# The account that orders the instructions of a two-stack transformer kernel charges each operation another duration

## The chip, the cores and the metric

The kernel runs on one NeuronCore of a Trainium2 chip. A core has five engines with instruction streams of their own: TensorE (PE, the matrix multiplier), VectorE (DVE), ScalarE (ACT), GpSimd (POOL) and SyncE (SP, which here only issues transfers). Each engine works through its instructions strictly in the order in which they were built, and an instruction that has to wait for another engine holds up everything behind it on its own. The metric is the device time of one launch in microseconds (us).

## The reference, cut to what matters

Two stacks are computed one after the other, in float32, on 512 tokens of 1024 channels (`second` gets the output of `first`, and 256 context tokens of its own).

```python
# first stack: two layers
x = x + gated_deltanet(rmsnorm(x), ...)      # layer 0: projections, a causal convolution of 4 taps,
                                             # chunks of 64 tokens, a triangular solve, a scan over 8 chunks
x = x + swiglu(rmsnorm(x), w_in, w_out)
x = x + dilated_attention(rmsnorm(x), ...)   # layer 1: 3 groups of 8 heads
x = x + swiglu(rmsnorm(x), w_in, w_out)

# second stack: two layers, each
h, hc = modulate(x, ...), modulate(ctx, ...)             # layer norm, scale and shift
qa, ka, va, zb, qc, kc, vc = split(h @ w_in)             # the same for hc
o_a = neighbourhood_attention(qa, ka, va, context, rpb)  # 6 heads
o_b = spatial_gating(gelu(zb), w_s, b_s, g_sgu)
o_c = attend(rope(rms(qc) * g_q), rope(rms(kc) * g_k), vc, context)
y = concat(rms(o_a), rms(o_b), rms(o_c)) @ w_o           # layer 0: also for the context
x = layer_norm(ALPHA * x + gate * y) ...                 # then a gated swiglu of the same kind
```

## The kernel before, in words

All activations stay on the chip, in blocks of 128 tokens (blocks 0 to 3 are the tokens, 4 and 5 the context). Weights are streamed in slabs of half a megabyte. A float32 product is made of three passes over rounded parts: `xh` times `wh`, `xl` times `wh`, `xh` times `wl`, where `h` is the rounded part of a number and `l` the rest. So each tile that goes into a product must first be rounded (ACT, `xh<-xn`) and have its rest taken (POOL, `xl<-xn,xh`), and each weight slab as well (ACT `whia`, `whib`; POOL `wloa`, `wlob`).

In time the program has eight stages: the gated delta net (0 to 440 us of the span), a feed-forward (to 870), the dilated attention (to 1130), a feed-forward (to 1480), the mixing sublayer of the second stack's first layer (to 1985), its feed-forward (to 2500), the mixing sublayer of its second layer (to 2905) and its feed-forward (to the end).

The order of the instructions is decided while the program is built, by the class `Weave`. The main thread writes the large products. Everything else is written by side chains, Python generators that are advanced a step at a time: a norm, a convolution, a softmax, a rotation. After every second matmul or so of a large product the main thread calls `tick`, which advances each side chain whose last result is ready, by the account, at least `MARGIN` (1000 ns) before PE's present time. The account is a clock for each engine, `t[PE]`, `t[DVE]`, `t[ACT]`, `t[POOL]`, and a time `ready` for each chain: `note` adds what `cost` charges for the instruction and, behind it, the hand-over `LAT`, which counts only where the chain's next instruction is on another engine. Where the main thread needs the result of a chain it calls `join`, and `advance` moves PE's clock on. No duration is measured at run time: a larger charge makes the account believe that a result comes later, so the chain's next step is written behind more matmuls. After this the tile framework still moves some instructions by a few places.

The places that the prediction speaks of: in the delta net, `conv` (line 680: three multiply-adds `kT<-m,cw,kT` that read a bank of PSUM, which the next large product needs), `blocks` (line 831: a recurrence of pairs `tmp<-Pk,T` and `T<-T,tmp`), `gram` (line 786); in the mixing sublayer, `modulate` (line 1773: `xn`, transposes `s<-ident,xn` on PE, scaling on ACT and DVE, `xh`, `xl`), `rope_T` (line 2107: `w2k` and its reciprocal root `rs_t`, `qrs` on DVE, then transposes `s<-ident,w2k` on PE), the tables `tqk` made from a load `w2k<-rope` (in `mix`, line 2025), `values` (line 2215) and `merge` (line 2195). All instructions pass through one helper and so have line 138 in the profile.

Of the kernel before, what the change touches and what calls it, by code (L numbers as in the profile page):

```python
# [121 lines left out]
def _free(ap):  # L122
    n = 1
    for s in ap.shape[1:]:
        n *= s
    return n
# [35 lines left out]
class Weave:  # L162


    LAT = 125.0
    MARGIN = 1000.0

    def __init__(self):
# [3 lines left out]
    def cost(self, e, op, a, k):  # L172
        out = a[0] if a else k["out"]
        if op == "dma_start":
            return "DMA", 2100.0 + _free(out) * 4 * out.shape[0] / 170.0
        if e == "PE":
            if op == "transpose":
                return e, 116.0
            n = _free(out)
            if a[1].dtype == F32R:  # L180
                return e, max(n * 0.4225, 116.0)
            return e, 1.7 * n
        n = max(_free(x) for x in a[:2] if hasattr(x, "shape"))
        if e == "DVE":
            return e, (75 if n < 64 else 120) + 1.04 * n
        if e == "ACT":
            return e, 100 + 0.85 * n
        return e, 100 + 2.2 * n

    def note(self, e, op, a, k):  # L190
        if e == "SP" and self.cur is None:
            return
        e, c = self.cost(e, op, a, k)
        s, t = self.cur, self.t
        if s is None:
            if e == "DMA":
                return
            t[e] = (t[e] if e == "PE" else max(t[e], t["PE"])) + c
        elif e == "DMA":
            s.ready += c  # L200
            s.eng = e
        else:
            start = t[e] if s.eng == e else max(t[e], s.ready)
            t[e] = start + c
            s.ready = t[e] + self.LAT
            s.eng = e

    def now(self):
# [2462 lines left out]
```

## Time and profile before

| | us |
|---|---|
| median of three runs | 3285.81 (3278.48 to 3289.23) |
| the profiled execution's own time | 3274.1 |
| its span | 3272.3 |
| PE busy | 3073.1 (94%) |
| DVE busy | 1633.1 (50%) |
| ACT busy | 1255.7 (38%) |
| POOL busy | 1705.2 (52%) |

The median is 11.7 us (0.36%) above the profiled execution, so sums made against the profile are carried over to the median as differences. Busy shares are means over eight stages; what a changed order is worth is to be read where PE, the busiest engine, stands still.

### The profile page before, as it was taken

The numbers are of one execution on the slowest core, as the hardware profiler recorded it, in microseconds if no ns is written. First come the engines' busy times: TensorE is split into PE (matmuls) and PEld (weight loads), VectorE is DVE, ScalarE is ACT, GpSimd is POOL, SyncE is SP. The second block draws the span as 40 slices with busy tenths as digits, with TensorE's granted clock in tenths as the row PEclk, the third lists the DMA queues.
The fourth block names the chain that finished last, engine by engine and source line by source line (L and its number), as shares of the span: only waits on it lengthen the run. The fifth ranks groups of instructions, "written<-read, shape, count | busy, mean of one in ns | idle before, by whom it ended". The sixth has DMA issues, their size and how long they took to land.

```text
span 3272.3 us, 46609 instructions
## 1 busy us (share of the span) xinstructions
PE 3073.1 (94%) x16596; PEld 2662.7 (81%) x16596; DVE 1633.1 (50%) x4221; ACT 1255.7 (38%) x2542; POOL 1705.2 (52%) x2163
## 2 busy tenths in 40 slices
PE   7899899999999899998998879999998899979997
PEld 6787788888999788888898768888887798868886
DVE  6886476666455674517546752021115855731113
ACT  4443332223444432235546534212122656452322
POOL 3424368774333396765534245444546624475665
PEclk9989899999999999999998889999999899989999
DMA  3212245553222455622111221122121112143231
GB/s 111 67 35 71 85 157 184 168 173 103 74 65 62 159 181 190 202 97 75 59 33 52 62 77 53 64 65 65 65 65 52 59 32 68 57 148 97 97 97 65
DMA packets 99467, 301.97 MB, mean 92 GB/s; under 512 B 18673, under 2 KB 26017, under 8 KB 99233
## 3 DMA queue, kind: packets, MB, share of 16 engines
q1 hardware_dynamic: 74000, 236.36, 22.3%
q10 hardware_dynamic: 25232, 62.62, 6.1%
q8 instruction: 131, 2.15, 0.3%
q14 instruction: 104, 0.84, 0.1%
HBM read 290.98 MB, written 7.95 MB: 91 GB/s over the span
## 4 chain that ended last, share of the span: by engine, by line
PE 54%; DVE 5%; ACT 2%; POOL 2%; issue 1%; DMA 1%; SPq 0%; ACTq 0%; DVEq 0%; POOLq 0%
PE b L138 28%; PE m L138 23%; PE s L138 4%; ACT xn L138 1%; DVE rs_t L138 1%; DVE w2k L138 1%; DVE x L138 1%; POOL wloa L138 0%; POOL xl L138 0%; DVE qrs L138 0%; ACT w2k L138 0%; POOL wlob L138 0%; DVE macc L138 0%; DVE xl L138 0%; DMA gr<-grow 0%
## 5 line engine op out<-in xcount | busy, mean ns | idle before, releaser
L138 POOL TENSOR_TENSOR wloa<-wrawa,whia 128x256 fp32r<-128x256 f32 x639 | 492.7, 802 | 515.8 <-ACT whia L138 479.2
L138 POOL TENSOR_TENSOR wlob<-wrawa,whib 128x256 fp32r<-128x256 f32 x475 | 364.6, 801 | 209.3 <-ACT whib L138 183.4
L138 DVE SCALAR_TENSOR_TENSOR th<-th,b 128x512 f32<-128x512 f32 x66 | 45.4, 687 | 611.1 <-ACT th L138 611.1
L138 ACT CAST whia<-wrawa 128x1024 fp32r<-128x1024 f32 (+2 forms) x164 | 168.2, 1027 | 379.6 <-PE m L138 202.8
L138 PE MATMUL m<-xh,whia 128*128 128x512 f32 (+1 forms) x760 | 269.8, 361 | 15.5 <-ACT xh L138 6.9
L138 PE MATMUL m<-xl,whia 128*128 128x512 f32 (+1 forms) x760 | 266.8, 357 | 13.9 <-POOL xl L138 13.8
L138 POOL TENSOR_TENSOR wloa<-wrawb,whia 128x256 fp32r<-128x256 f32 x232 | 192.2, 859 | 149.5 <-ACT whia L138 141.9
L138 ACT CAST whib<-wrawa 128x1024 fp32r<-128x1024 f32 (+1 forms) x123 | 125.5, 1022 | 350.4 <-PE m L138 162.0
L138 DVE SCALAR_TENSOR_TENSOR macc<-mw,cv,macc 128x1024 f32<-128x1024 f32 x140 | 235.1, 1719 | 9.2 <-DMA mw<-w_mod 8.8
L138 POOL TENSOR_TENSOR wlob<-wrawb,whib 128x256 fp32r<-128x256 f32 x239 | 192.4, 835 | 89.8 <-ACT whib L138 89.0
L138 PE MATMUL b<-xh,whib 128*128 128x512 f32 (+1 forms) x624 | 228.4, 372 | 1.4 <-ACT xh L138 1.4
L138 PE MATMUL b<-xl,whib 128*128 128x512 f32 (+1 forms) x624 | 227.4, 371 | 0.0
L138 PE MATMUL b<-xl,whia 128*128 128x512 f32 (+1 forms) x528 | 197.6, 378 | 2.8 <-POOL xl L138 2.8
L138 PE MATMUL b<-xh,whia 128*128 128x512 f32 (+1 forms) x528 | 198.0, 379 | 0.5 <-ACT xh L138 0.5
L138 POOL TENSOR_TENSOR hl<-th,hh 128x512 fp32r<-128x512 f32 (+1 forms) x110 | 158.1, 1446 | 69.8 <-ACT hh L138 67.3
L138 PE MATMUL m<-xh,wloa 128*128 128x512 f32 (+1 forms) x760 | 185.3, 354 | 0.0
L138 PEld LDWEIGHTS m<-xh,whia 128*128 128x128 f32 x760 | 145.4, 192 | 45.0 <-issue 8.4
L138 PEld LDWEIGHTS m<-xl,whia 128*128 128x128 f32 x760 | 145.2, 191 | 40.8 <-POOL xl L138 14.6
L138 PE MATMUL m<-whia,xh 128*128 128x512 f32 (+3 forms) x440 | 168.1, 385 | 5.7 <-ACT xh L138 3.2
L138 PE MATMUL m<-whib,xh 128*128 128x512 f32 (+3 forms) x432 | 162.1, 377 | 10.1 <-ACT xh L138 5.4
L138 PE MATMUL m<-whia,xl 128*128 128x512 f32 (+3 forms) x440 | 166.2, 380 | 3.8 <-POOL xl L138 3.3
L138 PE MATMUL m<-whib,xl 128*128 128x512 f32 (+3 forms) x432 | 161.7, 376 | 6.1 <-POOL xl L138 5.9
(457 smaller groups left out, 8043.3 us busy)
## 6 DMA issues: line engine op xcount, KB each, us to landing
mw<-w_mod ACTq DMA_DIRECT2D x96, 512.0 KB, 4.3
wrawa<-ffn_w_in SPq DMA_DIRECT2D x60, 512.0 KB, 3.4
wrawa<-w_ffn_in SPq DMA_DIRECT2D x56, 512.0 KB, 3.4
wrawa<-gdn_w_in SPq DMA_DIRECT2D x32, 512.0 KB, 3.4
wrawb<-w_ffn_in SPq DMA_DIRECT2D x32, 512.0 KB, 3.4
wrawa<-w_ffn_out SPq DMA_DIRECT2D x32, 512.0 KB, 3.4
wrawb<-ffn_w_in SPq DMA_DIRECT2D x28, 512.0 KB, 3.4
wrawa<-ffn_w_out SPq DMA_DIRECT2D x28, 512.0 KB, 3.5
```

The costliest lines, as they stand in the source:

```text
L138: r = f(*a, **k)
```

## The change

Two tables of numbers in `Weave` change. The hand-over, 125 ns behind every engine, becomes 250 ns behind PE and 60 ns behind the others. The fixed charge of an operation rises: on DVE from 75 ns (under 64 elements) or 120 ns to 155 ns, and 85 ns more with a running sum; on ACT from 100 to 150 ns, 60 ns more where the bias or the scale is a tile and 190 ns more with a running sum; on POOL from 100 to 180 ns. The charge of an element hardly changes (ACT 0.85 to 0.87 ns, POOL 2.2 to 2.18 ns, DVE 1.04 ns as before); PE's and the transfers' charges stay. No instruction is added or removed.

```diff
-    LAT = 125.0
+    LAT = {"PE": 250.0}
@@ cost()
-            return e, (75 if n < 64 else 120) + 1.04 * n
+            return e, 155 + 1.04 * n + (85 if total else 0)
         if e == "ACT":
-            return e, 100 + 0.85 * n
-        return e, 100 + 2.2 * n
+            vec = any(hasattr(k.get(x), "shape") for x in ("bias", "scale"))
+            return e, 150 + 0.87 * n + (60 if vec else 0) + (190 if total else 0)
+        return e, 180 + 2.18 * n
@@ note()
-            s.ready = t[e] + self.LAT
+            s.ready = t[e] + self.LAT.get(e, 60.0)
```

What this moves is seen in the built order. The four feed-forward stages keep theirs but for a few places at their seams, and the dilated attention nearly so. In the delta net and in both mixing sublayers large parts of it move. Three places follow.

The first is DVE in the delta net, about 130 to 135 us into the span of before: `T_282` and `tmp` are the recurrence of the first pair of heads, whose steps get shorter as it goes on (128x25x2, 128x24x2, ... 128x16x4, 128x15x5), and `qT<-m,cw,qT` is the convolution for the third pair. Before:

```order
L138 TENSOR_TENSOR T_282<-T_282,tmp 128x16x4
L138 TENSOR_TENSOR tmp<-Pk,T_282 128x75
L138 TENSOR_TENSOR T_282<-T_282,tmp 128x15x5
L138 SCALAR_TENSOR_TENSOR qT<-m,cw,qT 128x511
L138 TENSOR_TENSOR tmp<-Pk,T_282 128x70
L138 SCALAR_TENSOR_TENSOR qT<-m,cw,qT 128x510
L138 TENSOR_TENSOR T_282<-T_282,tmp 128x14x5
L138 SCALAR_TENSOR_TENSOR qT<-m,cw,qT 128x509
```

Now:

```order
L138 TENSOR_TENSOR T_282<-T_282,tmp 128x25x2
L138 TENSOR_TENSOR tmp<-Pk,T_282 128x48
L138 SCALAR_TENSOR_TENSOR qT<-m,cw,qT 128x511
L138 TENSOR_TENSOR T_282<-T_282,tmp 128x24x2
L138 SCALAR_TENSOR_TENSOR qT<-m,cw,qT 128x510
L138 TENSOR_TENSOR tmp<-Pk,T_282 128x69
L138 SCALAR_TENSOR_TENSOR qT<-m,cw,qT 128x509
```

The convolution stood behind the step of 15 and stands behind the step of 25 now, ten steps of the recurrence (twenty instructions) earlier against it.

The second is PE at the start of the first mixing sublayer: `m` are the products of a block with the weights of its keys and values (two slabs, `whia_111` with `wloa_112`, then `whia_109` with `wloa_110`), and `s<-ident,w2k` the transposes at the end of the rotation of context block 4. Before, all 24 products of block 0 and all 24 of block 1 stand ahead of it:

```order
L138 MATMUL m<-whia_109,xh_12034 128x256
L138 MATMUL m<-whia_109,xl_12035 128x256
L138 MATMUL m<-wloa_110,xh_12034 128x256 x4
L138 MATMUL s<-ident,w2k 128x128 x2
L138 MATMUL s<-ident,xn 128x128 x4
L138 MATMUL m<-whia_111,xh_12034 128x256
```

Now only the products with the first slab do:

```order
L138 MATMUL m<-whia_111,xh_12034 128x256
L138 MATMUL m<-whia_111,xl_12035 128x256
L138 MATMUL m<-wloa_112,xh_12034 128x256 x4
L138 MATMUL s<-ident,w2k 128x128 x2
L138 MATMUL m<-whia_109,xl_12035 128x256
L138 MATMUL m<-whia_109,xh_12034 128x256
```

So 23 products of the second slab have moved from ahead of the rotation's transposes to behind them. On POOL the rest `xl` of each block's second half has moved behind the rotation's multiplication by `g_k` in the same way.

The third is POOL at the start of the second mixing sublayer: `xl1` are rests of the context (`xn_21154` before and `xn_21191` now is block 5), `xl0` those of the tokens, and `tqk` the tables that need the load of `rope`. Before:

```order
L138 TENSOR_TENSOR xl1_21002<-xn_21091,xh1_21001 128x4x128 x2
L138 TENSOR_TENSOR xl1_21002<-xn_21154,xh1_21001 128x4x128 x2
L138 MEMSET zero_21335 128x1
L138 MEMSET va_21323 64x768
L138 TENSOR_TENSOR tqk_21337<-w2k_21342,g_q_21338 128x256
L138 TENSOR_TENSOR tqk_21337<-w2k_21342,g_k_21340 128x256
L138 TENSOR_TENSOR xl0_21000<-xn_21284,xh0_20999 128x4x128
L138 TENSOR_TENSOR tqk_21337<-w2k_21342,w2k_21344 128x256 x2
```

Now:

```order
L138 TENSOR_TENSOR xl1_21000<-xn_21091,xh1_20999 128x4x128 x2
L138 MEMSET zero_21337 128x1
L138 MEMSET va_21325 64x768
L138 TENSOR_TENSOR xl1_21000<-xn_21191,xh1_20999 128x4x128
L138 TENSOR_TENSOR tqk_21339<-w2k_21344,g_q_21340 128x256
L138 TENSOR_TENSOR tqk_21339<-w2k_21344,g_k_21342 128x256
L138 TENSOR_TENSOR tqk_21339<-w2k_21344,w2k_21346 128x256 x2
L138 TENSOR_TENSOR xl1_21000<-xn_21191,xh1_20999 128x4x128
L138 TENSOR_TENSOR xl0_20998<-xn_21288,xh0_20997 128x4x128 x2
```

The rest of block 5's second half stood ahead of the four table multiplications and stands behind them now, and so does the first half of block 0. On PE the transposes of block 5 have moved behind all 24 products of block 4, and on ACT the seven loads (the fifth is `rope`) ahead of the rounding of block 5's second half.

## Rows read from the trace of the kernel before

**Rows 1.** The page's head and its part on busy time.

```profile
span 3272.3 us, 46609 instructions
...
PE 3073.1 (94%) x16596; PEld 2662.7 (81%) x16596; DVE 1633.1 (50%) x4221; ACT 1255.7 (38%) x2542; POOL 1705.2 (52%) x2163
```

**Rows 2.** The page's chain of waits, by engine.

```profile
PE 54%; DVE 5%; ACT 2%; POOL 2%; issue 1%; DMA 1%; SPq 0%; ACTq 0%; DVEq 0%; POOLq 0%
```

**Rows 3.** Windows by stage: length, busy PE, PEld, DVE, ACT, POOL, clock, DMA share, GB/s.

```profile
0.00:440.00 440.00, 389.37 (x2350) 327.87 (x2350) 301.08 (x797) 184.64 (x463) 163.28 (x211) 0.95 0.23 77
440.00:870.00 430.00, 429.03 (x2001) 364.16 (x2000) 266.04 (x371) 132.94 (x203) 297.37 (x318) 1.00 0.47 149
...
1480.00:1985.00 505.00, 447.49 (x2729) 407.30 (x2728) 308.70 (x1097) 269.19 (x682) 213.20 (x342) 0.91 0.18 57
...
2500.00:2905.00 405.00, 352.64 (x2160) 318.91 (x2158) 275.54 (x940) 221.68 (x515) 199.91 (x293) 0.92 0.22 68
```

**Rows 4.** Groups of instructions: count, busy us, mean ns of one, idle before.

```profile
L138 DVE SCALAR_TENSOR_TENSOR th<-th,b 128x512 f32<-128x512 f32 x66 | 45.4, 687 | 611.1 <-ACT th L138 611.1
...
L138 DVE TENSOR_SCALAR rs_t<-rs,rs_x 128x1 f32<-128x1 f32 x138 | 36.0, 268 | 2.0
...
L138 POOL TENSOR_TENSOR wloa<-wrawa,whia 128x256 fp32r<-128x256 f32 x638 | 492.3, 803 | 503.6 <-ACT whia L138 479.2 <-PE m L138 20.6 <-issue 3.0
```

**Rows 5.** Windows of 20 us in the delta net.

```profile
120.00:140.00 20.00, 15.23 (x73) 11.74 (x72) 18.12 (x47) 9.20 (x26) 5.67 (x9) 1.00 0.23 79
140.00:160.00 20.00, 16.93 (x73) 13.11 (x71) 19.51 (x61) 7.88 (x12) 9.08 (x12) 1.00 0.27 86
```

**Rows 6.** Timeline of PE in the delta net: start, us, instruction, idle before.

```profile
127.41 0.47 PE L138 MATMUL m<-xh,whia 128*128 128x512 f32 x1 [1.78 <-DVE T L138]
...
155.03 0.47 PE L138 MATMUL m<-xh,whia 128*128 128x512 f32 x1 [1.34 <-DVE cx L138]
```

**Rows 7.** Timeline of DVE at the start of the first mixing sublayer.

```profile
1504.94 0.29 DVE L138 TENSOR_REDUCE qss<-w2k 128x2 f32<-128x128 f32 x1 [0.82 <-ACT w2k L138]
...
1509.43 1.21 DVE L138 SCALAR_TENSOR_TENSOR qrs<-rs_t,qrs 128x2 f32<-128x2 f32 x1
...
1513.59 0.16 DVE L138 TENSOR_TENSOR rs_t<-rs_t,rs_x 128x2 f32<-128x2 f32 x1
```

**Rows 8.** Timeline of POOL in the same stretch.

```profile
1506.85 3.77 POOL L138 TENSOR_TENSOR xl<-xn,xh 128x512 fp32r<-128x512 f32 x3
1512.30 0.46 POOL L138 TENSOR_TENSOR w2k<-w2k,g_k 128x128 f32<-128x128 f32 x1 [1.69 <-DVE rs_t L138]
```

**Rows 9.** Timeline of PE in the same stretch.

```profile
1517.48 0.44 PE L138 MATMUL s<-ident,w2k 128*128 128x128 f32 x2 [2.35 <-DVE xn L138]
```

**Rows 10.** Timeline of POOL at the start of the second mixing sublayer.

```profile
2534.35 2.52 POOL L138 TENSOR_TENSOR xl<-xn,xh 128x512 fp32r<-128x512 f32 x2 [2.90 <-ACT xh L138]
...
2544.92 0.72 POOL L138 TENSOR_TENSOR tqk<-w2k,g_q 128x256 f32<-128x256 f32 x1 [7.21 <-DMA w2k<-rope]
```

**Rows 11.** Timeline of PE in the same stretch.

```profile
2525.36 1.97 PE L138 MATMUL s<-ident,xn 128*128 128x128 f32 x8 [3.73 <-ACT xn L138]
...
2547.61 0.58 PE L138 MATMUL m<-whib,xl 128*128 128x256 f32 x1 [1.76 <-POOL xl L138]
```

**Rows 12.** Timeline of ACT's load of rope in the same stretch.

```profile
2541.14 0.44 ACTq L138 DMA_DIRECT2D w2k<-rope  x1
```

**Rows 13.** Windows at either clock in the same stretch.

```profile
2529.30:2534.60 5.30, 5.30 (x24) 5.24 (x24) 3.17 (x17) 3.02 (x7) 2.40 (x2) 0.50 0.08 26
2536.00:2538.50 2.50, 2.50 (x23) 2.50 (x22) 2.50 (x7) 2.07 (x2) 1.65 (x3) 1.00 0.00 0
```

**Rows 14.** Timeline of PE near the end of the first mixing sublayer.

```profile
1894.72 0.90 PE L138 MATMUL s<-ident,qa 128*128 128x128 f32 x3 [4.24 <-DVE qa L138]
```

**Rows 15.** Timeline of PE in the middle of the first mixing sublayer.

```profile
1849.73 1.11 PE L138 MATMUL b<-ident,w2k 128*128 128x128 f32 x4 [2.81 <-ACT w2k L138]
```

**Rows 16.** Timeline of PE near the end of the second mixing sublayer.

```profile
2861.34 0.55 PE L138 MATMUL s<-ident,qa 128*128 128x128 f32 x3 [2.20 <-DVE qa L138]
```

More of the change, by code (lines that the diff above doesn't have):

```diff
@@ L183, in cost @@
         n = max(_free(x) for x in a[:2] if hasattr(x, "shape"))
+        total = k.get("accum_out") is not None
         if e == "DVE":
-            return e, (75 if n < 64 else 120) + 1.04 * n
+            return e, 155 + 1.04 * n + (85 if total else 0)
         if e == "ACT":
-            return e, 100 + 0.85 * n
-        return e, 100 + 2.2 * n
+            vec = any(hasattr(k.get(x), "shape") for x in ("bias", "scale"))
+            return e, 150 + 0.87 * n + (60 if vec else 0) + (190 if total else 0)
+        return e, 180 + 2.18 * n
     def note(self, e, op, a, k):
```

## The prediction

> **What bounds the kernel now.** I read the page's busy times first. PE is busy 3073.1 of 3272.3 us [rows 1], and by the chain of waits the end also hangs on PE before any other engine, 54% against 5% for DVE [rows 2]. So a change of order can give back at most PE's idle time, 199.2 us, and costs whatever it adds to it. Where that time lies is told by the windows by stage [rows 3]: the feed-forward from 440 to 870 has 429.03 busy of 430.00, so nothing is to be had there (and its order stays); the delta net has 389.37 of 440.00 (50.6 idle, of which the start of the kernel is a part that no order changes), the first mixing sublayer 447.49 of 505.00 (57.5 idle), the second 352.64 of 405.00 (52.4 idle). These three stages, 160.5 us of idle PE, are also where the instructions move. The mixing sublayers show a granted clock of 0.91 and 0.92, against 1.00 in the feed-forward: beside the idle time they pay for stretches at 1.2 GHz. How dear these are is shown by two neighbouring stretches with the same kind of product [rows 13]: 24 instructions took 5.30 us at a granted clock of 0.50, 23 took 2.50 us at 1.00. A gap that is opened or closed is therefore worth up to about twice its length.
>
> **What the charges do.** The groups of instructions show how far the old charges were off [rows 4]: a multiply-add over 512 elements takes 687 ns (charged 120 + 532 = 652 before, 155 + 532 = 687 now), one step of a reciprocal root on one element 268 ns (76 before, 156 now), a POOL subtraction over 256 elements 803 ns (663 before, 738 now). But where a chain changes engine, the lower hand-over, 60 for 125 ns, takes back 65 of the 80 ns that a DVE operation gained. So chains that stay on DVE (the recurrence, the roots) are now held to be later, chains that hop from engine to engine about as late as before. No work is added, so each part below is a sum over PE's gaps.
>
> **Part 1, the delta net: -5 us.** From 120 to 160 us DVE is nearly full (18.12 and 19.51 of 20 us) and PE stands for 4.77 + 3.07 = 7.8 us [rows 5]. Most of that is four gaps ahead of the next large product, the first of 1.78 and the last of 1.34 us [rows 6]; at their mean, 1.56, they make 6.2 us. The product waits for a bank that a convolution on DVE has yet to read. In the new order the convolution stands ten steps of the recurrence earlier, so these gaps should nearly go. DVE does the same work in the same time, though: what is brought forward makes the recurrence late, and the transposes and solve behind it. I take -5, most of the four gaps. Below, it can be no better than the 7.8 us and a little of the clock, -10; above, if PE runs into the late recurrence by the length of the two convolutions put ahead of it (2 x 4 operations x 0.687 = 5.5), +5.
>
> **Part 2, start of the first mixing sublayer: +4 us.** PE came to the rotation's transposes of block 4 with all 48 products of blocks 0 and 1 done, and stood 2.35 us until 1517.48 [rows 9]. Now 23 of these products (2.5 us at full clock, 5.1 at half, by rows 13) stand behind the transposes, and PE waits there with work undone behind it: it comes some 3 us sooner, at 1512, waits, and still has the 23 to do. The chain on DVE that it waits for starts at 1504.94 [rows 7], and POOL's step of it at 1512.30 [rows 8]. It will be shorter than before. Its steps on two elements take 0.16 us at 1513.59 but 1.21 us at 1509.43 [rows 7], and the long ones lie beside the three subtractions that POOL does in 3.77 us from 1506.85 [rows 8]; two of those three have moved behind the chain, 2.5 us, in which a step now takes 0.16 instead of about 1.2, so the chain ends about 2.2 us sooner, near 1515.3. Then 0.4 for the transposes and about 4 for the 23 products makes 1519.7, where before everything was done at 1517.9: +1.8. Behind the 23 also stand the transposes of blocks 2 and 3, whose rests are then late by up to as much again; I take +4. Bounds: 0 (the shorter chain pays for all) and +9 (no shortening, all at half clock).
>
> The GPSIMD Engine Reference of the Trainium skill (Specifications) says that GpSimd's way into SBUF is shared with VectorE and that they get in each other's way when a DVE instruction has two SBUF inputs or runs in its two-port mode. That agrees with the rows just named, 1.21 against 0.16 us beside POOL's subtractions. It speaks against a fixed charge for DVE at all. By the rule alone the shorter chain would count in full and part 2 would be +2, and without it +6.
>
> **Part 3, start of the second mixing sublayer: +4 us.** On PE the transposes of block 5 ran at 2525.36 [rows 11]; they now follow all of block 4's products, which end at 2534.6 [rows 13], 9 us later. Scaling and rounding on ACT were ready only for POOL's subtraction at 2534.35 before [rows 10], so the first half loses some 5 us, not 9. POOL's second half now stands behind the tables, which waited until 2544.92 for the load [rows 10] that ACT issued at 2541.14 [rows 12], 3.8 us before. ACT issues it about 1 us sooner now, so the tables run from about 2544 to 2547 (4 x 0.72), the subtraction lands near 2548.3, and block 5's last 11 products come after that. Before, PE stood at that time too: block 0's products began at 2547.61, after a wait for POOL [rows 11]. So block 5 fills a gap that was there, and only the remainder, 2 to 5 us of products, is late, and block 1's half behind the rotation. I take +4; bounds 0 (all of it falls into the old gap) and +8 (the whole of the first half's delay and half of block 1's).
>
> **Part 4, end of the first mixing sublayer: -3 us.** PE stood 4.24 us ahead of the last merge [rows 14]. Now 10 more products of another block stand between; at the 0.214 us that one takes at full clock (429.03 / 2001, rows 3) they cover 2.1, and the clock has less cause to fall. Bounds -4 and 0.
>
> **Part 5, the middle of the mixing sublayers: +3 us.** Some waits get more cover, such as the 2.81 us for ACT at 1849.73 [rows 15], others less: several of the softmax chains in the first sublayer stand with 3 us of products between producer and consumer where there were 7 to 10. These chains are long, and I cannot price each. Bounds -6 (twice the gap shown) and +12 (the same number again in the other direction, doubled as at half clock). I take +3, nearer to zero than to the upper end, since each late chain also delays others that then wait less.
>
> **Part 6, the rest: 0.** Near the end of the second sublayer the 2.20 us [rows 16] are covered by 18 products (3.9 us), and block 1's second transposes go behind block 0's, which costs about as much: 0, between -2 and +2. The dilated attention and the feed-forwards keep their order.
>
> **The sum.** -5 + 4 + 4 - 3 + 3 + 0 = +3 us on the profiled execution's own 3274.1: 3277. The median of the runs shown is 11.7 higher, 3285.81, so the time to expect is 3289. All lower ends together are -22, all upper ends +36.
>
> **The rivals.** *The waits go.* The old charge of a DVE chain was a third of its price, so its consumers were written too early and PE stood; with the dearer charge they come later. For it: the delta net's gaps and the 2.81 and 4.24. Against it: chains that hop engines are charged as before, and most gaps of the mixing sublayers lie at starts and ends, where there is nothing to put between. Price: parts 1, 4 and 5 at their lower ends, 2 and 3 at +1 each: -10 - 4 - 6 + 2 = -18, so 3268.
> *POOL's queue stands.* In both starts a POOL instruction that waits (the tables for a load, 7.21 us [rows 10]; the multiplication for DVE, 1.69 us [rows 8]) now stands ahead of the rests that the products need. Once that wait ends later than PE's last product ahead of it, each us goes straight to the end, at half clock. Price: parts 2 and 3 at +9 and +8, 4 more for the products done at 0.50, the others as taken (-5): +16, so 3302. Against it: PE stood there anyway.
> *It charges what no trace shows.* A step that takes 0.16 or 1.21 us is charged 157 ns either way. The order is then another, not a better one, and the parts cancel: 3286.
>
> **How the numbers follow.** A measurement of this kernel can tell about 0.3% from no change, 9.9 us. My forecast and the last rival both lie within that; with their spread they hold 0.37. Faster by more, the first rival and the lower tail: 0.31. Slower, POOL's queue and the upper tail: 0.32. For 8 times in 10 I go to -26 and +31 around the median: 3260 to 3317, which leaves out about a tenth on either side; the forecast's own range is 3276 to 3296.
>
> **What would show it.** Part 1: the four gaps between 120 and 160 us gone and DVE still full. Part 2: PE's wait ahead of the rotation's transposes longer than 2.35, the steps of 1.2 us fewer. Part 3: POOL's tables ahead of a subtraction, and PE waiting for `xl` after block 4's products. Part 4: the 4.24 below 2.2. It is wrong if the feed-forwards differ, or if the delta net and the mixing sublayers all move in one direction by more than 10 us.

## The result and the profile after

The changed kernel takes 3319.82 us (median of six runs, 3316.45 to 3323.68), the kernel before, in the same series, 3276.89 (3273.59 to 3289.23). The ratio is 1.0122, with a 95% interval of 1.011 to 1.0134: slower by 42.9 us between the medians (the ratio is taken by rounds; 1.22% of 3276.89 is 40 us, so differences in us are good to a few us). The forecast was no change (+3 us), its range ended at 3317, and slower by over 0.3% had a chance of 0.32. The sum was wrong by 40 us: even all upper ends of its parts together, +36, don't reach what was measured.

The page's rows on the span, the busy times and the chain, in the changed kernel [rows 1, 2]:

```profile
span 3321.9 us, 46617 instructions
...
PE 3097.9 (93%) x16596; PEld 2686.5 (81%) x16596; DVE 1643.5 (49%) x4221; ACT 1259.3 (38%) x2542; POOL 1711.5 (52%) x2163
...
PE 54%; DVE 5%; ACT 3%; POOL 2%; DMA 1%; issue 1%; ACTq 0%; SPq 0%; DVEq 0%; POOLq 0%
```

The span grew by 49.6 us (its own time is 3323.68, the slowest of its six). Every engine ran the same number of instructions of work, yet PE is busy 24.8 us longer, and idle 224.0 instead of 199.2, which is another 24.8. So in these two executions half of the loss is waiting, and the other half is products that took longer: the mean granted clock is 0.966 in the one and 0.957 in the other. That isn't chance of the two: in the executions that list it, it is 0.961 to 0.966 for the kernel before (26 of the first series of experiments) and 0.955 to 0.958 in all six of the changed kernel. The chain alone would hide it: it has hardly changed.

Where it lies is told by the windows by stage, cut at the same PE instructions as in [rows 3]; the third is the dilated attention. The columns are length, busy PE, PEld, DVE, ACT, POOL, granted clock, DMA share and GB/s.

```profile
0.00:445.90 445.90, 393.12 (x2349) 332.29 (x2350) 305.44 (x798) 184.99 (x462) 164.12 (x211) 0.94 0.23 77
445.90:877.00 431.10, 429.67 (x2004) 364.70 (x2003) 263.55 (x375) 134.04 (x203) 299.89 (x318) 1.00 0.46 148
877.00:1147.90 270.90, 249.16 (x1369) 227.73 (x1368) 158.50 (x555) 122.07 (x301) 91.83 (x123) 0.94 0.28 87
1497.70:2008.00 510.30, 450.11 (x2740) 406.62 (x2739) 307.04 (x1099) 273.27 (x688) 215.49 (x343) 0.92 0.17 56
2523.00:2954.60 431.60, 365.55 (x2170) 333.96 (x2169) 276.08 (x940) 221.49 (x514) 196.36 (x291) 0.89 0.21 64
```

The dilated attention in the kernel before, which the prediction gave no row:

```profile
870.00:1130.00 260.00, 243.54 (x1372) 222.25 (x1371) 159.37 (x559) 122.79 (x301) 91.48 (x123) 0.97 0.28 90
```

The PE instruction of the same rank in PE's order, taken in the middle of each feed-forward, comes later by +5.9 us behind the delta net, by 11.8 more behind the dilated attention, by 5.3 more behind the first mixing sublayer and by 26.6 more behind the second: 49.6, all of it. These are differences of two single executions, and the last section shows how far such a one can be off. The second mixing sublayer went from 405 to 431.6 us, and its granted clock from 0.92 to 0.89.

**The delta net.** Windows of 20 us, of the changed kernel [rows 5], and the two long waits of PE behind them [rows 6]:

```profile
120.00:140.00 20.00, 19.53 (x104) 15.93 (x103) 19.45 (x59) 7.91 (x24) 9.09 (x13) 1.00 0.14 54
140.00:160.00 20.00, 13.62 (x65) 10.82 (x64) 18.03 (x47) 8.54 (x25) 8.37 (x12) 1.00 0.24 79
160.00:180.00 20.00, 15.52 (x134) 14.31 (x135) 17.74 (x57) 6.75 (x17) 2.08 (x2) 0.69 0.11 34
```

```profile
145.47 0.47 PE L138 MATMUL m<-xh,whia 128*128 128x512 f32 x1 [3.46 <-DVE cx L138]
...
162.10 1.70 PE L138 MATMUL s<-Uc,kT 32*32 32x32 f32 x32 [5.02 <-DVE T L138]
```

In the kernel before, the window from 160 us was:

```profile
160.00:180.00 20.00, 17.74 (x169) 16.28 (x169) 16.32 (x51) 7.16 (x26) 2.82 (x4) 0.74 0.08 27
```

The gaps are gone from 120 to 140 us (19.53 busy for 15.23), but not from 140 to 160 (13.62 for 16.93): there PE stands 3.46 us for another convolution (`cx`), and from 157 us for the recurrence `T`, which gave its place to the convolution and is late. That wait is 5.02 us. The products behind it run in a window with a granted clock of 0.69; it was low there before as well, 0.74.

**The first mixing sublayer.** PE at its start and near its end [rows 9, 14]:

```profile
1520.69 1.97 PE L138 MATMUL s<-ident,xn 128*128 128x128 f32 x8 [3.84 <-ACT xn L138]
...
1532.52 0.44 PE L138 MATMUL s<-ident,w2k 128*128 128x128 f32 x2 [1.60 <-DVE w2k L138]
...
1915.87 0.90 PE L138 MATMUL s<-ident,qa 128*128 128x128 f32 x3 [3.13 <-DVE qa L138]
```

The wait ahead of the rotation's transposes is shorter than before (1.60 for 2.35), and the 4.24 is 3.13; one of 3.84 us has opened ahead of a block's transposes.

**The second mixing sublayer.** PE at its start [rows 11] and in its middle:

```profile
2545.61 0.58 PE L138 MATMUL m<-whib,xh 128*128 128x256 f32 x1 [3.96 <-ACT xh L138]
2550.39 0.58 PE L138 MATMUL m<-whib,xl 128*128 128x256 f32 x1 [4.20 <-POOL xl L138]
...
2568.86 0.58 PE L138 MATMUL m<-whib,xl 128*128 128x256 f32 x1 [2.33 <-POOL xl L138]
...
2789.82 1.11 PE L138 MATMUL b<-ident,w2k 128*128 128x128 f32 x4 [4.45 <-ACT w2k L138]
```

The windows around the 4.45:

```profile
2766.00:2786.00 20.00, 19.38 (x120) 18.84 (x119) 9.76 (x44) 11.32 (x26) 11.39 (x19) 1.00 0.19 61
2786.00:2806.00 20.00, 16.18 (x78) 16.18 (x79) 13.98 (x77) 10.90 (x30) 8.99 (x18) 0.58 0.25 78
2806.00:2826.00 20.00, 13.55 (x81) 11.36 (x81) 17.21 (x85) 14.76 (x45) 5.69 (x11) 0.84 0.19 62
```

Up to 2786 PE is full, at full clock. Then it stands 4.45 us for a softmax chain (`w2k` on ACT), and the 20 us behind it run at a granted clock of 0.58, in which 78 instructions of PE ran where 120 ran in the window ahead. In the built order 175 large products stood between the first and the last score product of this sublayer's neighbourhood attention, and 100 do now. The experiments below show that this number by itself doesn't set the loss.

Its end is the other place. PE's waits in this sublayer, summed by what was waited for (us in all, times, longest), in the changed kernel:

```profile
PE s L138 <- ACT xn L138: 27.1, 5, 15.1
...
PE b L138 <- ACT w2k L138: 7.9, 5, 4.4
```

and in the kernel before (where waits of the second kind make 0.3 us from 2740 to 2800):

```profile
PE s L138 <- ACT xn L138: 15.3, 5, 6.3
```

The longest of them is ahead of the next norm's transposes. PE, then POOL ahead of it, in the changed kernel:

```profile
2921.59 1.12 PE L138 MATMUL s<-ident,xn 128*128 128x128 f32 x4 [15.11 <-ACT xn L138]
2925.50 1.97 PE L138 MATMUL s<-ident,xn 128*128 128x128 f32 x8 [2.80 <-ACT xn L138]
```

```profile
2905.59 2.78 POOL L138 TENSOR_TENSOR wloa<-wrawb,whia 128x256 fp32r<-128x256 f32 x4
2908.34 4.75 POOL L138 TENSOR_TENSOR wloa<-wrawa,whia 128x256 fp32r<-128x256 f32 x4
2913.05 1.26 POOL L138 TENSOR_TENSOR x<-x,vc 128x512 f32<-128x512 f32 x1
2914.27 3.75 POOL L138 TENSOR_TENSOR wlob<-wrawa,whib 128x256 fp32r<-128x256 f32 x4
2917.98 1.25 POOL L138 TENSOR_TENSOR x<-x,vc 128x512 f32<-128x512 f32 x1
```

A block's residual sum (`x<-x,vc`) stands behind eight weight splits, the next behind four more, and DVE has the statistics of these blocks written among the norm's roots of the others. But of the 15.11 us DVE waits only a small part for POOL (us in all, times, longest):

```profile
DVE bst L138 <- POOL x L138: 2.7, 2, 2.2
```

For 12.32 us of the 15.11 it is busy, with the steps of several norms in turn. So no block's norm ends early, and PE stands 15.11 us for the first transposes; eight more begin at 2925.50. In the kernel before, two residual sums stood behind eight splits as well, but the first eight transposes came after 2.16 us. The longest wait was that of the next eight:

```profile
2870.82 1.09 PE L138 MATMUL s<-ident,xn 128*128 128x128 f32 x8 [2.16 <-ACT xn L138]
...
2878.21 1.97 PE L138 MATMUL s<-ident,xn 128*128 128x128 f32 x8 [6.29 <-ACT xn L138]
```

### The profile page after: what moved, and what is told of

It reads as the page before. It is cut to its first block, busy times and chain, and to the rows that moved or that the text cites. A ratio compares the mean times of both kernels' runs of the same rounds, so it can differ in the third digit from the quotient of the medians.

```text
span 3321.9 us, 46617 instructions
## 1 busy us (share of the span) xinstructions
PE 3097.9 (93%) x16596; PEld 2686.5 (81%) x16596; DVE 1643.5 (49%) x4221; ACT 1259.3 (38%) x2542; POOL 1711.5 (52%) x2163
## 4 chain that ended last, share of the span: by engine, by line
PE 54%; DVE 5%; ACT 3%; POOL 2%; DMA 1%; issue 1%; ACTq 0%; SPq 0%; DVEq 0%; POOLq 0%
PE b L138 28%; PE m L138 23%; PE s L138 4%; ACT xn L138 1%; DVE rs_t L138 1%; DVE w2k L138 1%; DVE x L138 1%; ACT w2k L138 1%; POOL wloa L138 1%; POOL wlob L138 0%; ACT xh L138 0%; DVE qrs L138 0%; ACT qs L138 0%; DMA gr<-grow 0%; POOL xl L138 0%
## 5 line engine op out<-in xcount | busy, mean ns | idle before, releaser
L138 POOL TENSOR_TENSOR wloa<-wrawa,whia 128x256 fp32r<-128x256 f32 x639 | 501.5, 816 | 469.0 <-ACT whia L138 428.6
```

Of the source, the lines that this page charges most:

```text
L138: r = f(*a, **k)
```

## The experiments

All were timed in three rounds against the kernel before on the same chip (its medians were 3280.83, 3277.65 and 3278.16 in the three series); ratios stand with their 95% interval.

**Is it one place or many?** A flag `new` picks the old or the new charges and hand-overs, so that one stage is ordered by the new account and the rest by the old one (`new` is set ahead of the delta net, of the dilated attention with the feed-forward in front, of the first or of the second mixing sublayer). Theory A: each stage has a price of its own, as the profile's shifts show it, and the prices add up. Theory B: they don't. By the traces, the delta net and the dilated attention are then ordered exactly as in the changed kernel; of the 2729 and 2160 PE instructions of the first and the second mixing sublayer, 271 and 653 stand in other places than there, since the account comes to these stages with other clocks.

```diff
+    new = False
@@ cost()
+        if not self.new:
+            if e == "DVE":
+                return e, (75 if n < 64 else 120) + 1.04 * n
+            if e == "ACT":
+                return e, 100 + 0.85 * n
+            return e, 100 + 2.2 * n
@@ note()
-            s.ready = t[e] + self.LAT.get(e, 60.0)
+            s.ready = t[e] + (self.LAT.get(e, 60.0) if self.new else 125.0)
```

The delta net alone:

> The changed charges and hand-overs hold only while the delta net is written, the old ones in all later stages. Theory A (each stage's new order has its own price, and the prices add up): PE's work stood 5.9 us later at the end of the delta net in the changed kernel, so +6 us on before, with the first 140 us of the span faster by about 8 as in the changed kernel and the following 40 slower by about 13. Theory B (one thing is paid once and carried on, such as weights that arrive later): the loss of the later stages comes along too, +20 us or more.

Measured: 3288.04 us, 1.0026 (1.0013 to 1.0039), +7.2 us.

The dilated attention alone:

> The changed account holds only while the first feed-forward and the dilated attention are written. Theory A: +12 us, the shift that built up between 780 and 1120 us of the span of before. Theory B (the dilated attention lost only because the delta net before it came later): within 3 us of before.

Measured: 3285.59 us, 1.0014 (1.0003 to 1.0024), +4.8 us. Less than the 11.8 of the profile, and theory B's 3 us lie in the interval (1 to 8 us).

The first mixing sublayer alone:

> The changed account holds only from the second feed-forward to the end of the first mixing sublayer. Theory A: +5 us (17.7 to 23.0 us of shift in the changed kernel). Theory B: within 3 us of before.

Measured: 3290.91 us, 1.0032 (1.002 to 1.0044), +10.1 us, twice the profile's shift.

The second mixing sublayer alone:

> The changed account holds only from the third feed-forward to the end of the program, so of the parts that move only in the second mixing sublayer. Theory A: +27 us (23.0 to 49.6 us of shift), with PE's wait of 15.1 us ahead of the last feed-forward's transposes. Theory B: under +13 us.

Measured: 3296.93 us, 1.0047 (1.0029 to 1.0064), +16.1 us: the dearest, as expected, but 10 below the shift, and theory B's 13 us lie in the interval (10 to 21 us). The wait of 15.1 us is not in it: ahead of the last feed-forward's transposes PE stands 3.27, 3.05 and 3.03 us.

The four excesses, 0.26 + 0.14 + 0.32 + 0.47, make 1.19%; the whole change costs 1.22%. The sum speaks for theory A; the sizes of single stages, taken from one profiled execution, are off by up to 10 us, and by themselves two of the four runs don't exclude theory B.

**Was the kernel before a lucky order?** Theory C: it was, and any other order costs some 1%. Theory D: the loss lies in what the account says, and in the charges rather than in the hand-over. Four kernels tell: the old account with a margin of 1010 for 1000 ns, which gives another order in the delta net and in both mixing sublayers but hardly another account; the new charges alone; the new hand-over alone; and the new account with a margin of 990.

```diff
-    MARGIN = 1000.0
+    MARGIN = 1010.0
```

> The kernel before, old charges and hand-overs, with a MARGIN of 1010 instead of 1000 ns: one percent of a number that is a guess anyway, but 4457 lines of PE's order differ (6848 in the changed kernel). Theory C (the order of before is one well-chosen draw, and nearly any other order loses): +10 to +35 us. Theory D (the new charges are what makes it slower, since they write consumers later and so lengthen chains that nothing hides): within 5 us of before.

Measured: 3276.43 us, 0.9995 (0.9983 to 1.0007), no change. Its busy times by the page:

```profile
PE 3073.3 (94%) x16596; PEld 2663.0 (81%) x16596; DVE 1638.7 (50%) x4221; ACT 1254.7 (38%) x2542; POOL 1706.6 (52%) x2163
```

PE's busy time is that of before within 0.2 us [rows 1], in an order in which 4457 lines differ on PE alone (compared place by place in the traces, by tile name and shape, 1733 of PE's 16596 instructions, against 4848 in the changed kernel). So theory C falls as it was put, with nearly any other order: this one costs nothing. It is one order, and a near one; each order farther off that is tried below costs 0.5% or more.

The new account with the other margin (`MARGIN = 990.0`):

> The changed kernel with a MARGIN of 990 ns (1745 lines of PE's order differ from the changed kernel's). Theory D: the changed kernel's time within 5 us, +38 to +48 on before. Theory C: another draw of the same kind, anywhere from +15 to +50, and the long wait ahead of the last feed-forward may go.

Measured: 3315.55 us, 1.0111 (1.0092 to 1.0131), +38 us: this neighbour of the new account is as slow as itself, and the wait ahead of the next norm is there again (15.10 us for 15.11).

The charges alone (`cost` of the changed kernel, `LAT` of the kernel before):

```diff
-    LAT = {"PE": 250.0}
+    LAT = 125.0
@@ note()
-            s.ready = t[e] + self.LAT.get(e, 60.0)
+            s.ready = t[e] + self.LAT
```

> The new charges with the old hand-over of 125 ns everywhere, so that every chain is held to be later than in either kernel. Theory D: the loss of the changed kernel or more, +40 to +60 us, since the charges push and the lower hand-overs no longer take back. Theory C: another draw, +10 to +45.

Measured: 3299.19 us, 1.0059 (1.0044 to 1.0075), +21.5 us.

The hand-over alone (`LAT` of the changed kernel, `cost` of the kernel before):

> The new hand-overs (250 ns behind PE, 60 behind the others) with the old charges. Theory D: chains are held to be earlier on the whole, so no loss or a gain, -15 to +5 us. Theory C: another draw, +5 to +35.

Measured: 3302.8 us, 1.0063 (1.0044 to 1.0082), +25 us. Theory D's ranges are missed by both halves, and theory C's hold both; what speaks against C is the pair of neighbours at 1010 and 990. Each half costs about half, and 0.59 + 0.63 = 1.22%, the whole; in us the two medians add to 46.7, against 42.9.

**Too late, or out of balance?** Theory E: both halves make the account hold chains to be later than the old one did, so their steps are written behind more products, these run out, and PE stands at the end of a stage. Then a larger margin with the old account costs too, PE's hand-over of 250 does most of the second half, and a smaller margin brings the new account back. Rival F: what counts is how the engines stand to each other; a common delay does little.

The old account with `MARGIN = 1400.0`:

> The kernel before with a MARGIN of 1400 instead of 1000 ns: every step of every side chain is written about 400 ns of PE's time later, with the old charges and hand-overs. Theory E (lateness: each step that is written later uses up main products as cover ahead of it, and at the end of a stage the chains are left over with nothing beside them): +20 to +50 us, mostly in the mixing sublayers. Theory F (not how late but in which order the chains follow one another, by their charges relative to each other): within 8 us of before.

Measured: 3297.96 us, 1.0053 (1.0036 to 1.0071), +20 us, with one mark of the change: PE busy 20.1 us longer with the same instructions. By its profile the loss builds up in the two mixing sublayers (15.2 and 14.3 us between the feed-forwards, nothing ahead of them), as theory E said; the long wait ahead of the next norm is not there (5.91 us).

```profile
PE 3093.2 (94%) x16596; PEld 2682.1 (81%) x16596; DVE 1645.9 (50%) x4221; ACT 1255.4 (38%) x2542; POOL 1704.2 (52%) x2163
```

PE's hand-over alone, everything else as before:

```diff
-    LAT = 125.0
+    LAT = {"PE": 250.0}
@@ note()
-            s.ready = t[e] + self.LAT
+            s.ready = t[e] + self.LAT.get(e, 125.0)
```

> Old charges; only the hand-over behind PE rises from 125 to 250 ns, the others stay at 125. Theory E: this is the half of the hand-over change that makes steps later, so it has all of its loss, +15 to +30 us. Theory F: the falling hand-overs behind the other engines have their share, so +12 at most.

Measured: 3294.08 us, 1.0048 (1.0034 to 1.0061), +16 us. Theory F's 12 us lie in the interval (11 to 20 us). Longer waits ahead of the next norm come with this one number; the sum over the second mixing sublayer, of the kind shown above:

```profile
PE s L138 <- ACT xn L138: 25.9, 6, 10.0
```

Set against the 25 us of the whole hand-over, some 9 are left for the others' fall from 125 to 60 ns; that is a difference of two runs, not a run, and not clear of noise (0.63 and 0.48%, with intervals that overlap).

The new account with `MARGIN = 600.0`:

> The changed kernel with a MARGIN of 600 ns, so that its chains are written about as early as before in spite of the larger charges. Theory E: most of the loss comes back, -10 to +15 us against before. Theory F: the loss stays, +30 to +45.

Measured: 3303.0 us, 1.0072 (1.0055 to 1.009), +25 us. About 18 of the 43 come back, the other 25 don't: neither E nor F had that. PE's busy time is back at 3.6 us over before, but idle time is not:

```profile
PE 3076.7 (93%) x16596; PEld 2663.9 (81%) x16596; DVE 1636.7 (50%) x4221; ACT 1252.3 (38%) x2542; POOL 1701.6 (52%) x2163
```

Its end of the second mixing sublayer, PE and then POOL, has the same picture as above, and a longer wait:

```profile
2901.35 1.12 PE L138 MATMUL s<-ident,xn 128*128 128x128 f32 x4 [17.90 <-ACT xn L138]
```

```profile
2881.56 3.74 POOL L138 TENSOR_TENSOR wloa<-wrawb,whia 128x256 fp32r<-128x256 f32 x4
2885.26 4.87 POOL L138 TENSOR_TENSOR wloa<-wrawa,whia 128x256 fp32r<-128x256 f32 x4
2890.09 1.26 POOL L138 TENSOR_TENSOR x<-x,vc 128x512 f32<-128x512 f32 x1
2891.31 3.75 POOL L138 TENSOR_TENSOR wlob<-wrawa,whib 128x256 fp32r<-128x256 f32 x4
2895.03 1.25 POOL L138 TENSOR_TENSOR x<-x,vc 128x512 f32<-128x512 f32 x1
```

The old account with `MARGIN = 700.0`, to see whether earlier is simply better:

> The kernel before with a MARGIN of 700 ns: every step 300 ns earlier. If the lateness of theory E had no other side, this would be faster, -20 to -5 us; if before stands where lateness and waits balance, or by theory F, within 8 us or slower, since PE meets results that are not there yet.

Measured: 3300.11 us, 1.0067 (1.0045 to 1.0089), +22 us. Earlier costs as much as later, and in another way:

```profile
PE 3076.9 (93%) x16596; PEld 2664.2 (81%) x16596; DVE 1639.6 (50%) x4221; ACT 1254.4 (38%) x2542; POOL 1700.9 (52%) x2163
```

PE's busy time is 3.8 us over before, the rest is idle time. Counted in the trace from the first product on, it has 126 gaps of 0.3 us or more where the kernel before has 110, and as many of 2 us or more as that (25). The late orders have 31 (margin 1400) and 33 (the change) of these long ones. So the old account with its 1000 ns stood in a valley. On its late side PE is busy longer and the clock is lower (20.1 us, 0.958 for 0.966, margin 1400); on its early side nearly all is idle time (20.4 us, margin 700). The number of long gaps alone doesn't tell the sides apart: the order with a margin of 1010, which costs nothing, has 28. No kernel tried is faster than the kernel before.

The new account with a margin of 600 has the marks of this early side: PE busy 3.6 us longer and idle 24.0, with 125 gaps of 0.3 us or more. So 600 may be past the bottom of the new account's own valley. No margin between 600 and 990 was run with it, and how much of the 25 us a better margin would bring back is open. By the code of `note` and `tick` a smaller margin isn't the counterpart of larger charges either: charges and hand-overs add up from step to step along a chain, and the margin comes on top once, whatever the length of the chain. So 400 ns less make short chains earlier than before and can leave long ones late; no run tells the two apart.

**Does the stock of products tell the loss?** One stretch of the second mixing sublayer answers that from the traces: the PE instructions that ran from 2740 to 2840 us in the kernel before, and those of the same rank in other kernels, with the number of large products between the first and the last score product. In turn: before (175 products), the change (100), the charges alone (180), the new account with a margin of 600 (99).

```profile
2740.19:2840.08 99.89, 92.44 (x573) 83.23 (x573) 75.01 (x358) 63.80 (x173) 43.71 (x77) 0.95 0.22 68
2770.26:2880.64 110.38, 99.12 (x575) 91.40 (x573) 77.98 (x364) 64.41 (x176) 41.59 (x75) 0.85 0.20 61
2747.87:2859.87 112.00, 99.88 (x574) 91.10 (x573) 72.46 (x336) 60.33 (x164) 46.41 (x81) 0.85 0.21 66
2754.85:2854.12 99.27, 88.84 (x573) 81.83 (x573) 75.18 (x361) 62.69 (x173) 41.10 (x74) 0.91 0.22 68
```

The stretch is 10.5 us longer with 100 products and 12.1 us longer with 180, and no longer with 99. So the number of products between the scores isn't the cause. The loss here comes with the new charges at a margin of about 1000 ns: it is 14.2 us at 990, 11.2 with only this sublayer changed, and 1.7 with the hand-over alone. These are single executions; with the order of the kernel before, the same stretch took 6.3 us longer in one of them (clock 0.87) and no longer in another.

## Why the prediction was wrong, point by point

- **The bound**, PE, was right, and so, in the sum, was that a gap costs up to twice its length: 24.8 us idle came with 24.8 us of slower products. In single stretches it cost more: from 2740 to 2840 us 10.5 us with 3.8 more of idle time.
- **What the charges do** was half right. That "chains that hop from engine to engine" are held to be "about as late as before" left out PE's own hand-over, 125 to 250 ns behind every product that a chain waits for. By itself that costs 16 us. The sentence priced the two halves of the change against each other; measured, they add (0.59 and 0.63%).
- **Part 1** (-5, bounds -10 and +5): the mechanism was right on both sides, the net wrong. Between 130 and 135 us the same products came some 8 us sooner, as said. That was lost again, and more: 5 us by 150, behind the wait of 3.46, and by 182, behind the wait of 5.02 for the late recurrence, the large products came 2.6 us later than before, and 5.9 at the stage's end. So what is paid behind the gain is 10 to 14 us, not at most 5.5: the bound held only the length of the convolutions. Net +5.9 in the profile, +7.2 alone.
- **Part 2** (+4): PE is 4.0 us late at 1540, but not for the reason given. The predicted longer wait is shorter, 1.60. A wait of 3.84 ahead of the transposes of another block stands in that stretch instead; how much of the 4.0 it makes wasn't isolated.
- **Part 3** (+4): +2.5 at 2570 and some 6 at 2580, between its bounds and by the mechanism given. The transposes of block 5 no longer stand in the wait for block 4's rest, which is 4.20 us now, and behind block 4's products PE waits 2.33 us for the `xl` that POOL does after the tables.
- **Part 4** (-3): the wait is 3.13, not below 2.2. The stretch around it (1850 to 1900 us) is 5.2 us shorter by the same ranks on PE, but it is 3.8 us shorter as well in the two executions that keep this stage's order (only the delta net, only the second mixing sublayer changed). So what is left for the part is 1 to 2 us, and not clear of that scatter.
- **Part 5** (+3, bounds -6 and +12) is the step that failed most: the middle of the mixing sublayers, which it priced by the one wait that I could see there, 2.81 [rows 15], with the late and the covered waits taken to cancel. In the second sublayer they don't: its middle costs 15 us (4.6 from 2570 to 2740, 10.5 from there to 2840), with the waits for the softmax chains (7.9 us for 0.3) and the clock behind them (0.85 for 0.95). The same stretches cost 16 to 18 us in the three other runs with the new charges at a margin near 1000. The middle of the first sublayer (1540 to 1850) is 4.6 us longer, but that shows nothing: it is 5.9 and 6.5 us longer in the two executions with its order unchanged, and there is no more idle time in it than before. A common stock of products, of which each later chain takes more as cover until the last find none (175 among the scores before, 100 now), would explain it, but the stretch compared above contradicts that. Why just these chains come late is open.
- **Part 6** (0) failed as well. "The dilated attention and the feed-forwards keep their order" held for the feed-forwards (shift 0.0). The dilated attention differs in some 45 places; it costs 4.8 us alone (11.8 in the profile). The end of the second sublayer was given 0 for its wait of 2.20 [rows 16]; it costs 9 in the profile, 7 of them idle (27.0 for 19.9 us between the same ranks on PE, 2840 to 2925 us of before): the 15.11 ahead of the next norm has taken the place of waits of 2.16, 6.29, 2.68 and 5.42, which I had not looked at.

In sum, against the profile's 49.6: the middle of the second sublayer is short by some 12, the dilated attention by 12, Part 1 by 11 and the end of the second sublayer by 9; the rest, some 3, lies within the scatter of two executions. The rival that "POOL's queue stands" had the right sign and the wrong place (PE's wait behind the tables is 2.33 us); the one that "the waits go" forecast a gain. The third, that another order comes out the same, holds for the margin of 1010 and not for the change.

What the runs settle: by rounds the loss is spread over the four stages that are ordered anew (0.26, 0.14, 0.32 and 0.47%) and over both halves of the change; a margin 10 ns to the side leaves either kernel near its time (0.9995, and +38 for +43 us); and a common delay of 400 ns costs as much as either half (+20 us). What stays open is which property of an order makes it slow. Neither the number of products among the scores nor lateness alone tells it: at a margin of 600 25 of the 43 us remain, and whether that is the balance between engines or a margin that is too small by now was not run. That POOL's splits ahead of the residual sums hold up the next norm explains a small part only: DVE's wait for these sums is 2.7, 2.7 and 3.5 us in the three executions with the long wait (15.11, 15.10 and 17.90), and no run took the splits out by themselves.

## What to carry to other kernels

With the old charges and hand-overs, a margin of 700 or 1400 ns costs as much as either half of the change: a planner's charges and its margin belong together. To correct one of them towards the trace moves every chain, so it has to be tried with the margin scanned anew, which was done here at two values only (600 and 990), and even then need not pay. Price a change of order by stages, and look for changed places in all of them, at their ends too, and not only at the gaps that are visible now. And before a stretch that got longer is explained, look at it in an execution that kept its order.

## What the runs showed that was not expected

A schedule can lose as much in busy time as in idle time with not one instruction of work more: +24.8 us of each. And an unchanged order isn't an unchanged duration. The second mixing sublayer in the profile of the run in which only the dilated attention is ordered anew,

```profile
2511.10:2926.70 415.60, 360.00 (x2158) 326.27 (x2157) 279.15 (x940) 220.96 (x515) 199.82 (x292) 0.90 0.21 66
```

took 10.6 us more than in [rows 3] (405.00, with 352.64 busy and a clock of 0.92), with the same order. The delta net, ordered as in the changed kernel in both, came out 5.9 us longer than before in the changed kernel's profile and 12.6 in that of the run with only the delta net changed. So a stage's shift between two single executions is good to about 10 us, and only the rounds tell less than that.

The steps of the rotation's root on DVE, in the changed kernel, and POOL's subtraction beside them [rows 7, 8]:

```profile
1529.40 1.22 DVE L138 TENSOR_TENSOR rs_t<-rs_t,rs_x 128x2 f32<-128x2 f32 x1
1530.65 0.16 DVE L138 SCALAR_TENSOR_TENSOR qrs<-rs_t,qrs 128x2 f32<-128x2 f32 x1
```

```profile
1529.31 1.29 POOL L138 TENSOR_TENSOR xl<-xn,xh 128x512 fp32r<-128x512 f32 x1
```

A step on two elements takes 0.16 us, and 1.22 where it starts just behind a POOL subtraction of 1.29: it ends when that does, as if it had waited for all of it. The two durations are almost a factor of eight apart, so a fixed charge for the step can be right in one of the two places at most.
